# State space stage of a two-block network: the recurrence of two groups at once in complex pairs

## The chip, the cores and the metric

The kernel runs on one core of one Trainium2 chip. The metric is the device time of the program in microseconds, and the kernel before is given as the median of 3 runs. The program has one core, so the slowest core is that core.

## The reference

The network has an attention block and a state space block, each with a normalization behind it, and further parts in the same program. The change lies in the state space block (S5). Its reference, cut to what is computed there:

```python
E_BRANCH, S5_GROUP, S5_GROUPS, S5_STATE, S5_CHUNK = 2048, 16, 128, 64, 128

def _s5_direction(u_ctx, u_lat, lam, dt, bmat, cmat):
    lam_dt = lam * dt[:, None]
    lam_bar = jnp.exp(lam_dt)
    b_bar = ((lam_bar - 1.0) / lam)[..., None] * bmat
    ...
    def step(h, u_chunk):
        bu = jnp.einsum('btgs,gps->btgp', u_chunk.astype(jnp.complex64), b_bar)
        a = jnp.broadcast_to(lam_bar, bu.shape)
        _, xs = lax.associative_scan(_ssm_combine, (a, bu), axis=1)
        xs = xs + powers[None] * h[:, None]
        y = jnp.einsum('btgp,gsp->btgs', xs, cmat).real
        return xs[:, -1], y
    ...
    h_ctx, y_ctx = run(u_ctx, h0)
    _, y_lat = run(u_lat, h_ctx)

def _s5_mixer(h_lat, h_ctx, w_in, ...):
    u_l, g_l = jnp.split(h_lat @ w_in, 2, axis=-1)
    u_c, g_c = jnp.split(h_ctx @ w_in, 2, axis=-1)
    ...
    y = jax.nn.gelu(y)
    ya, yb = jnp.split(y @ w_glu + b_glu, 2, axis=-1)
    return ((ya * jax.nn.sigmoid(yb)) * jax.nn.silu(g)) @ w_out
```

For two directions a linear recurrence x(t) = lam x(t-1) + B u(t) with complex lam runs over 256 context tokens and goes on over 256 latent tokens (backwards for the second direction), and only the latents' output is wanted.

## The kernel before

The kernel does the recurrence in steps of 8 tokens, so a direction has 32 columns of context and 32 of latents. The 2048 channels lie in four rounds or groups b = 0 to 3 of 16 blocks of operators, worked in four parts a = 0 to 3 of 1 MB each. For a round:

- **Linears.** `u` computes 128 columns of the input branch for context and latents (48 matmuls; a weight part is split into a high and a low half, `weight`: a load on SyncE, a cast on ScalarE at L97, a difference on VectorE at L98). `s5_store_u` copies the result with ScalarE (`s_ut`, L438), turned so that 8 tokens lie in a column, and stores it to DRAM (`d_u`); `s5_load_u` reads it back as U (L446) with another partition order. The first round's U is read on SyncE, the others' on GpSimd's queue.
- **Blocks.** `s5_blocks` multiplies U by the operators `d_rt` (matmuls `vps`, L472, 256 a round), and ScalarE copies each of 8 results to V (L475), which holds [real/imaginary][direction][16 rows][64 columns] on 128 partitions.
- **Scan.** `s5_scan` is VectorE's part: a tree of five levels over the context's columns (the first in two halves), then 7 steps of 4 columns and 3 steps of 8 over the latents, with a table of powers of lam (`s5_steps`, L332 to L337). A step is two products (L493), one sum (L495), one difference (L496), one sum (L497). At the end the second direction's columns are turned (L517).
- **Out.** `s5_out` multiplies U ("within", L536, operators `d_t`) and the states V ("across", L549, operators `d_o`), transposes (`ytps`, L560), and ScalarE does the gelu (L1096). The gates (`lin`, 24 matmuls each) are linears whose silu is stored for later.

TensorE and VectorE run in the order in which the code is written. `s5_layer` writes it: round b's scan is handed out in pieces (`run(scan, us)`) beside the linears of later rounds, the gates, and the within and across products of round b-1; then the blocks of round b+1 come, and the next scan. Operators lie in a ring of five 1 MB tiles, loaded on GpSimd's queue; weight parts in a ring of two (high and low). Behind the stage, `ya` in two halves feeds the GLU's linears.

## Time and profile before

| | us |
|---|---|
| median of 3 runs | 1450.82 |
| lowest and highest | 1448.18, 1453.40 |
| profiled execution, its own time | 1449.68 |
| span of the trace | 1447.9 |
| TensorE busy, whole span | 1328.2 (92%) |
| VectorE busy, whole span | 1150.6 (79%) |
| ScalarE busy, whole span | 712.2 (49%) |

The profile is of one execution. The span is what the trace covers of that execution's own time. Busy shares are means over stages that differ: in the state space stage, some 240 of the 1448 us, VectorE and TensorE both have a large share, and which of them sets the end is read from that stage alone.

### The profile page before, as it was taken

To read this page: it belongs to the slowest core of one execution; us is meant where nothing else is said; L and a number is where in the kernel's file an instruction comes from. 1 tells how busy PE (TensorE), PEld (TensorE's weight loads), DVE (VectorE), ACT (ScalarE), POOL (GpSimd) and SP (SyncE) were. 2 spreads that over 40 slices of the span, in tenths; PEclk is the share of its full clock that TensorE was granted. 3 is DMA by queue.
4 is the path that set the end of the run, shared out by engine and by line. 5 is a ranking of instruction groups with operands and counts; after the bars stand their busy time and mean duration, and the time that the engine had idled before them with its cause. 6 is when DMAs were issued, how large, how long until landed. Compare 5 with 4: busy or idle time off the path is not lost.

```text
span 1447.9 us, 31095 instructions
## 1 busy us (share of the span) xinstructions
PE 1328.2 (92%) x12512; PEld 1196.9 (83%) x12512; DVE 1150.6 (79%) x2123; ACT 712.2 (49%) x1308; POOL 102.9 (7%) x225
## 2 busy tenths in 40 slices
PE   5879979999999988988768699999999999999997
PEld 4656657888888887888757599999998999999996
DVE  7999888998888899389898766555578876888887
ACT  4424436765656536322333264444347556655554
POOL 0012221111001100111111000000000000000000
PEclk9989988999999998999898899999999999999999
DMA  9469996665455544797778665655555453555552
GB/s 347 165 197 282 294 280 168 183 178 157 156 159 158 163 124 154 236 315 256 256 269 298 252 228 181 209 196 193 189 166 180 154 182 103 179 188 188 189 183 96
DMA packets 140625, 291.40 MB, mean 201 GB/s; under 512 B 30480, under 2 KB 70080, under 8 KB 135104
## 3 DMA queue, kind: packets, MB, share of 16 engines
q1 hardware_dynamic: 108592, 232.01, 48.2%
q0 software_dynamic: 11360, 49.34, 10.9%
q10 hardware_dynamic: 20528, 8.06, 2.1%
q8 instruction: 98, 1.61, 0.4%
q14 instruction: 47, 0.39, 0.1%
HBM read 234.83 MB, written 54.53 MB: 200 GB/s over the span
## 4 chain that ended last, share of the span: by engine, by line
PE 67%; DVE 20%; DMA 7%; issue 3%; ACT 3%; SPq 0%; DVEq 0%; ACTq 0%
PE lin L120 14%; PE lin L121 14%; PE lin L119 14%; DVE s_t L493 4%; DVE wl L98 3%; PE vps L472 2%; DVE s_V L495 2%; DMA sp_x<-in_s_bcw_dram 2%; DVE sp_t L37 2%; DMA mraw<-in_w_mod_dram 1%; PE dn L121 1%; PE dn L119 1%; PE dn L120 1%; DMA d_o<-sp_o 1%; DVE s_V L497 1%
## 5 line engine op out<-in xcount | busy, mean ns | idle before, releaser
L97 ACT CAST wh<-wr 128x1024 fp32r<-128x1024 f32 x268 | 280.7, 1049 | 405.4 <-PE lin L120 258.0
L98 DVE TENSOR_TENSOR wl<-wr,wh 128x1024 fp32r<-128x1024 f32 x268 | 327.6, 1223 | 146.3 <-ACT wh L97 145.6
L119 PE MATMUL lin<-prH,wh 128*128 128x256 f32 x512 | 145.3, 284 | 0.0
L119 PE MATMUL lin<-yaH,wh 128*128 128x256 f32 x512 | 144.9, 283 | 0.0
L120 PE MATMUL lin<-yaL,wh 128*128 128x256 f32 x512 | 144.7, 283 | 0.0
L121 PE MATMUL lin<-prH,wl 128*128 128x256 f32 x512 | 143.7, 281 | 1.0 <-DVE wl L98 1.0
L120 PE MATMUL lin<-prL,wh 128*128 128x256 f32 x512 | 144.1, 281 | 0.4 <-DVE prL L109 0.2
L121 PE MATMUL lin<-yaH,wl 128*128 128x256 f32 x512 | 144.2, 282 | 0.0
L120 PEld LDWEIGHTS lin<-prL,wh 128*128 128x128 f32 x512 | 96.6, 189 | 2.1 <-DVE prL L109 1.0
L119 PEld LDWEIGHTS lin<-yaH,wh 128*128 128x128 f32 x512 | 97.6, 191 | 0.0
L121 PEld LDWEIGHTS lin<-yaH,wl 128*128 128x128 f32 x512 | 97.5, 190 | 0.0
L119 PEld LDWEIGHTS lin<-prH,wh 128*128 128x128 f32 x512 | 96.7, 189 | 1.0
L120 PEld LDWEIGHTS lin<-yaL,wh 128*128 128x128 f32 x512 | 97.4, 190 | 0.0
L121 PEld LDWEIGHTS lin<-prH,wl 128*128 128x128 f32 x512 | 96.2, 188 | 1.2 <-DVE wl L98 1.2
L493 DVE TENSOR_TENSOR s_t<-s_V,s_tab 128x256 f32<-128x256 f32 (+2 forms) x120 | 73.1, 652 | 16.0 <-ACT s_V L475 14.7
L121 PE MATMUL u<-h,wl 128*128 128x256 f32 x224 | 64.1, 286 | 9.7 <-DVE wl L98 9.6
L121 PE MATMUL lin<-h,wl 128*128 128x256 f32 x128 | 43.2, 338 | 32.2 <-DVE wl L98 32.2
L427 POOL DMA_DIRECT2D d_t<-sp_g x128 | 67.0, 531 | 59.6 <-DVE sp_g L37 55.4
L119 PE MATMUL u<-h,wh 128*128 128x256 f32 x224 | 64.0, 286 | 0.0
L120 PE MATMUL u<-h,wh 128*128 128x256 f32 x224 | 63.3, 283 | 0.0
L119 PE MATMUL lin<-hH,wh 128*128 128x512 f32 x144 | 60.9, 423 | 0.7 <-ACT hH L103 0.7
L37 DVE TENSOR_TENSOR sp_t<-s_pb,sp_x 128x1024 f32<-128x1024 f32 x64 | 59.9, 953 | 0.6
(505 smaller groups left out, 3837.2 us busy)
## 6 DMA issues: line engine op xcount, KB each, us to landing
wr<-in_glu_dram SPq DMA_DIRECT2D x64, 512.0 KB, 3.3
wr<-in_w_up_dram SPq DMA_DIRECT2D x44, 512.0 KB, 3.3
wr<-in_w_in_dram SPq DMA_DIRECT2D x32, 512.0 KB, 4.8
mraw<-in_w_mod_dram SPq DMA_DIRECT2D x64, 256.0 KB, 3.3
d_rt<-sp_rt SPq DMA_DIRECT2D x64, 256.0 KB, 4.1
d_o<-sp_o SPq DMA_DIRECT2D x32, 512.0 KB, 4.7
wr<-in_s_in_dram SPq DMA_DIRECT2D x32, 512.0 KB, 4.4
s_op<-d_o POOLq DMA_DIRECT2D x16, 1024.0 KB, 7.3
```

Of the source, the lines that this page charges most:

```text
L37: return lambda *a, **k: self.net.in_order(f(*a, **k))
L97: self.in_order(nc.scalar.copy(hi, raw))
L98: self.in_order(nc.vector.tensor_tensor(lo, raw, hi.bitcast(F32), SUB))
L119: self.in_order(t.matmul(out, a[0], b[0], start=start, stop=False))
L120: self.in_order(t.matmul(out, a[0], b[1], start=False, stop=False))
L121: self.in_order(t.matmul(out, a[1], b[0], start=False, stop=stop))
L427: nc.gpsimd.dma_start(self.d_t[k].rearrange("s i j e c -> i s j e c")[:, :, j, e], a)
L472: self.in_order(nc.tensor.matmul(p[64 * e:64 * e + 64, c:c + 64], rt[:, d, j, r, 64 * e:64 * e + 64], u, start=True, stop=True, skip_group ...
L493: go(v.tensor_tensor(t[:, x], src.to_broadcast([128, 2, 32, n]), a[x].unsqueeze(1).to_broadcast([128, 2, 32, n]), MUL))
L495: go(v.tensor_tensor(dst, dst, t[:, 0], ADD))
L497: go(v.tensor_tensor(dst[:, 1], dst[:, 1], t[:, 1, 0], ADD))
```

## The change

- V holds pairs: real and imaginary part of a state lie side by side. The context's columns go to a tile C of the group, the latents' 31 columns and a start column to V of a pair of groups; ScalarE copies each block's result in two pieces (L476, L477), and turns the second direction in doing so.
- The context tree is one per group (`s5_context`): four levels, then one step for the last column only. The latents (`s5_latents`) go column by column, 31 steps, for two groups at once. A step (`s5_step`) is four operations, each on the result of the one before: product with the real part (L483), sum (L484), product of the swapped pair with the signed imaginary part (L483), sum (L484). The table of powers shrinks to doublings.
- The linears of rounds 1 to 3 and the gates come from one list (`linear`); weight parts are fetched two ahead while inputs are computed, every second one into a spare tile (`wx`). U is loaded on SyncE for all rounds, between the weight parts; the turned copy `s_ut` has one buffer instead of two; the operators' ring has four tiles instead of five.
- The order is made by two clocks, one of TensorE (`clock[0]`) and one of VectorE (`clock[1]`), that a table of costs moves on. What it makes on TensorE: one linear, then blocks(0,0) and so on, a linear and a block in turn to blocks(0,3); a linear; within(0) with a linear in it; blocks(1,0), a linear, blocks(1,1) to (1,3); then a linear and a part of blocks(2) in turn; three linears (the last input one and two gates), blocks(3) with a gate; across(0), across(1) and within(1) to (3) with gates between; behind the scan's end across(2) and across(3). Before, two linears came ahead of the four blocks of round 0, and across(3) alone stood behind the scan's end.

On VectorE, at the start of the scan. Before (`s_V` are the states, `wl` the low half of a weight part):

```order
L493 TENSOR_TENSOR s_t<-s_V,s_tab 128x512 x2
L495 TENSOR_TENSOR s_V<-s_V,s_t 128x64x8
L496 TENSOR_TENSOR s_V<-s_V,s_t 128x32x8
L497 TENSOR_TENSOR s_V<-s_V,s_t 128x32x8
L493 TENSOR_TENSOR s_t<-s_V,s_tab 128x512 x2
L495 TENSOR_TENSOR s_V<-s_V,s_t 128x64x8
L496 TENSOR_TENSOR s_V<-s_V,s_t 128x32x8
L497 TENSOR_TENSOR s_V<-s_V,s_t 128x32x8
L98 TENSOR_TENSOR wl<-wr,wh 128x1024
L493 TENSOR_TENSOR s_t<-s_V,s_tab 128x512 x2
L495 TENSOR_TENSOR s_V<-s_V,s_t 128x64x8
L496 TENSOR_TENSOR s_V<-s_V,s_t 128x32x8
```

and now, where group 1's context ends and the latents of groups 0 and 1 begin (`s_lam` and `s_li` are lam's parts):

```order
L483 TENSOR_TENSOR s_t<-s_C,s_tr 128x64
L484 TENSOR_TENSOR s_V<-s_C,s_t 128x2x16x2
L483 TENSOR_TENSOR s_t<-s_C,s_ti 128x64
L484 TENSOR_TENSOR s_V<-s_V,s_t 128x2x16x2
L483 TENSOR_TENSOR s_t<-s_V,s_lam_579 128x128
L484 TENSOR_TENSOR s_V<-s_V,s_t 128x2x32x2
L483 TENSOR_TENSOR s_t<-s_V,s_li 128x128
L484 TENSOR_TENSOR s_V<-s_V,s_t 128x2x32x2
L100 TENSOR_TENSOR wx<-wr,wx 128x1024
L483 TENSOR_TENSOR s_t<-s_V,s_lam_579 128x128
L484 TENSOR_TENSOR s_V<-s_V,s_t 128x2x32x2
L483 TENSOR_TENSOR s_t<-s_V,s_li 128x128
```

The steps of the latents have one column instead of four or eight, and weight parts (now L100) stand between them at other places.

On SyncE, behind the first operators. Before (`in_s_in` is the input weight, all of round 1 to 3's U loads stood on GpSimd's queue):

```order
L96 DMA wr<-in_s_in_dram 128x1024
L451 DMA s_op<-d_rt 128x2048 x2
L446 DMA s_U<-d_u 128x512 x4
L451 DMA s_op<-d_rt 128x2048 x2
L96 DMA wr<-in_s_in_dram 128x1024 x19
L96 DMA wr<-in_glu_dram 128x1024 x5
```

and now:

```order
L456 DMA s_op<-d_rt 128x2048 x2
L451 DMA s_U<-d_u 128x512
L98 DMA wr<-in_s_in_dram 128x1024 x3
L451 DMA s_U<-d_u 128x512
L98 DMA wr<-in_s_in_dram 128x1024 x2
L451 DMA s_U<-d_u 128x512 x2
L98 DMA wr<-in_s_in_dram 128x1024
L451 DMA s_U<-d_u 128x512
L98 DMA wr<-in_s_in_dram 128x1024
L451 DMA s_U<-d_u 128x512
L98 DMA wr<-in_s_in_dram 128x1024
L451 DMA s_U<-d_u 128x512
```

The U loads of rounds 1 to 3 stand between the weight parts.

On ScalarE at the end of the stage (`s_ysb` are a group's products, `y` the gelus, `yaH` their high half, `wh` the high half of a weight part). Before:

```order
L1096 ACTIVATE y<-ytps 128x128 x8
L1128 CAST yaH<-y 128x512 x2
L556 COPY s_ysb<-yps 128x32x16 x2
L97 CAST wh<-wr 128x1024
L1096 ACTIVATE y<-ytps 128x128 x8
L97 CAST wh<-wr 128x1024
L1128 CAST yaH<-y 128x512 x2
```

and now:

```order
L1158 ACTIVATE y<-ytps 128x128 x8
L1163 CAST yaH<-y 128x512 x2
L558 COPY s_ysb<-yps 128x32x16 x2
L1158 ACTIVATE y<-ytps 128x128 x8
L99 CAST wh<-wr 128x1024
L1163 CAST yaH<-y 128x512 x2
L99 CAST wh<-wr 128x1024 x2
```

The first GLU weight's cast stood ahead of the last eight gelus and stands behind them. And where linear (2,3) is turned and stored, ScalarE has the cast of the next weight part ahead of the turned copy.

The diff, cut to its core:

```diff
+    def s5_turn_u(self, ps, tp, bufs=2):
+        ut = tp.tile([128, 8, 2, 32], F32, name="s5_ut", bufs=bufs)
         for seg in range(2):
-            nc.scalar.copy(ut[:, :, 1 - seg, :], ps[:, seg * 256:seg * 256 + 256].rearrange("p (k s) -> p s k", s=8))
-        nc.scalar.dma_start(self.d_u[b, j].rearrange("s p k -> p s k")[:, ::-1], ut.rearrange("p s g k -> p s (g k)"))
-
-    def s5_load_u(self, b, j, tp, queue=None):
-
-        nc = self.nc
-        if j == 0:
-            self.U[b] = tp.tile([128, 4, 8, 64], F32, name="s5_U", bufs=3)
-        (queue or nc.gpsimd).dma_start(self.U[b][:, j].rearrange("p q k -> p (q k)"),
-                                       self.d_u[b, j].rearrange("s (i q) k -> (s i) (q k)", q=8))
+            self.nc.scalar.copy(ut[:, ::-1, 1 - seg, :],
+                                ps[:, seg * 256:seg * 256 + 256].rearrange("p (k s) -> p s k", s=8))
+        return ut
+    def s5_store_u(self, b, j, ps, tp, bufs=2):
+        self.nc.scalar.dma_start(self.d_u[b, j].rearrange("s p g k -> p s (g k)"),
+                                 self.s5_turn_u(ps, tp, bufs).rearrange("p s g k -> p s (g k)"))
+    def s5_load_u(self, b, j, U):
+        self.nc.sync.dma_start(U[:, j].rearrange("p q g k -> p (q g k)"),
+                               self.d_u[b, j].rearrange("s (i q) g k -> (s i) (q g k)", q=8))
...
-        t = self.ops.tile([128, 2048], F32, name="s5_op", bufs=5)
+        t = self.ops.tile([128, 2048], F32, name="s5_op", bufs=4)
...
-                nc.scalar.copy(V[:, :, d, 4 * a:4 * a + 4, :].rearrange("p r q k -> p r (q k)"),
-                               p.rearrange("p (r c) -> p r c", r=2))
...
-        def step(a, src, dst):
-
-            n = dst.shape[-1]
-            t = T[:, :, :, :, 0:n]
-            for x in range(2):
-                go(v.tensor_tensor(t[:, x], src.to_broadcast([128, 2, 32, n]),
-                                   a[x].unsqueeze(1).to_broadcast([128, 2, 32, n]), MUL))
-            go(v.tensor_tensor(dst, dst, t[:, 0], ADD))
-            go(v.tensor_tensor(dst[:, 0], dst[:, 0], t[:, 1, 1], SUB))
-            go(v.tensor_tensor(dst[:, 1], dst[:, 1], t[:, 1, 0], ADD))
...
+            pv = p.rearrange("p (r q k) -> p r q k", r=2, q=4)
+            c, x = (t[:, 4 * a:4 * a + 4].rearrange("p q k r -> p r q k") for t in (C[:, d], V[:, d, b % 2]))
+            nc.scalar.copy(c[:, :, :, ::-1] if d else c, pv[:, :, :, 0:32])
+            nc.scalar.copy(x[:, :, :, 1 - d:32 - d], pv[:, :, :, 32 + d:63 + d])
+    def s5_step(self, a, src, swapped, t, base, dst):
+        v = self.nc.vector
+        for x, y, z in ((src, a[0], base), (swapped, a[1], dst)):
+            self.in_order(v.tensor_tensor(t, x, y.to_broadcast(t.shape), MUL))
+            self.in_order(v.tensor_tensor(dst, z, t, ADD))
+    def s5_column(self, V, c, b=None, swap=False):
+        return bass.AP(tensor=V.tensor, offset=V.offset + 2 * c[0] + 1024 * (b or 0) + swap,
+                       ap=[V.ap[0], [2048 + 2 * (c[1] - c[0]), 2], [64, 32 if b is None else 16], [1 - 2 * swap, 2]])
+    def s5_context(self, b, C, V, tp):
+        Cf = C.rearrange("p d q k r -> p (d q) k r")
+        t = tp.tile([128, 1024], F32, name="s5_t")
+        for l in range(4):
             h, m = 1 << l, 2 << l
-            for c in (range(0, 32, 16) if l == 0 else (0,)):
-                e = c + 16 if l == 0 else 32
-                step(power(h), Vf[:, :, :, c + h - 1:e:m], Vf[:, :, :, c + m - 1:e:m])
-                yield 0.6 + 0.27 * ((e - c) // m)
-
-        for k in range(7):
-            step(power(1), Vf[:, :, :, 31 + k:63:8], Vf[:, :, :, 32 + k:63:8])
-            yield 1.5
-        for k in range(39, 63, 8):
-            step([self.tab[:, x, b] for x in range(2)], Vf[:, :, :, k - 1:k], Vf[:, :, :, k:k + 8])
-            yield 2.5
-
-        for r in range(2):
-            go(v.tensor_copy(V[:, r, 1, :, 0:31], V[:, r, 1, :, 62:31:-1]))
-        yield True
-
-    def s5_out(self, b, UVS, tp, emit):
+            a = self.tr[:, b, l].unsqueeze(2).unsqueeze(3), self.ti[:, b, l].unsqueeze(2)
+            i, o = slice(h - 1, 32, m), slice(m - 1, 32, m)
+            x, n = Cf[:, :, o], 32 // m
+            self.s5_step(a, Cf[:, :, i], Cf[:, :, i, ::-1],
+                         t[:, 0:64 * n].rearrange("p (c k r) -> p c k r", c=32, r=2), x, x)
+            yield 0.7 + 0.27 * n
+        x, base = (C[:, :, :, k] for k in (15, 31))
+        a = (self.tr[:, b, 4].rearrange("p (d c) -> p d c", d=2).unsqueeze(3),
+             self.ti[:, b, 4].rearrange("p (d c) r -> p d c r", d=2))
+        self.s5_step(a, x, x[:, :, :, ::-1], t[:, 0:64].rearrange("p (d c r) -> p d c r", d=2, r=2), base,
+                     self.s5_column(V, (0, 31), b % 2))
+        yield 0.9
+    def s5_latents(self, g, V, tp):
+        t = tp.tile([128, 1024], F32, name="s5_t")[:, 0:128].rearrange("p (d c r) -> p d c r", d=2, r=2)
+        a = (self.lam8[:, 0].rearrange("p (d c q) -> p d c q", d=2, c=2)[:, :, g].unsqueeze(3),
+             self.li[:, g].rearrange("p (d c) r -> p d c r", d=2))
+        for k in range(31):
+            c, o = (k, 31 - k), self.s5_column(V, (k + 1, 30 - k))
+            self.s5_step(a, self.s5_column(V, c), self.s5_column(V, c, swap=True), t, o, o)
+            yield 1.18
...
+                while len(parts) < n and asked[0] < len(linears):
+                    k, x = asked[0], linears[asked[0]]
+                    place = None
+                    if k < 12 and k % 2 == 1:
+                        place = [spare[:, k // 2 % 2, i] for i in range(2)]
+                    parts.append(self.weight(I["s5_in"][16 + x if isinstance(x, int) else 4 * x[0] + x[1]],
+                                             place=place))
+                    asked[0] += 1
+                    clock[1] += 1.3
...
+            def linear():
+                n = asked[0] - len(parts)
+                fetch(1)
+                w, x = parts.pop(0), linears[n]
+                fetch(2 if n < 10 else 1)
+                if isinstance(x, int):
+                    p = self.ps("lin")
+                    self.products(p[:, 0:256], w, (h1[0][:, 0], h1[0][:, 1]))
+                    sg = tp.tile([128, 256], F32, name="s5_sg", bufs=2)
+                    nc.scalar.activation(sg, p[:, 0:256], AF.Silu)
+                    nc.scalar.dma_start(self.d_sg[x][:, 0:256], sg)
+                    beside(2.9)
+                else:
+                    b, j = x
+                    if j == 0:
+                        U[b] = tp.tile([128, 4, 8, 2, 32], F32, name="s5_U", bufs=3)
+                    self.s5_store_u(b, j, self.u(w, h1), tp, 1)
+                    self.s5_load_u(b, j, U[b])
+                    beside(5.8)
...
+                if a == 3:
+                    clock[1] = max(clock[1], clock[0] + 1.0) if not jobs else clock[1]
+                    jobs.append(self.s5_context(b, C[b], V[b // 2], tp))
+                    if b % 2 == 1:
+                        jobs.append(self.s5_latents(b // 2, V[b // 2], tp))
...
+            U[0] = tp.tile([128, 4, 8, 2, 32], F32, name="s5_U", bufs=3)
+            for j in range(4):
+                self.s5_load_u(0, j, U[0])
+            ahead = [self.operator(self.d_rt[a], nc.sync) for a in range(4)]
+            self.ordered = (mybir.EngineType.PE, mybir.EngineType.DVE)
+            for a in range(4):
+                linear()
+                if a == 1:
+                    self.s5_steps(tp)
+                    clock[1] += 4.5
+                blocks(0, a)
+            linear()
+            within, across, close = out(0)
+            for a in range(4):
+                within(a)
+                if a == 1:
+                    linear()
+            blocks(1, 0)
+            linear()
+            for a in range(1, 4):
+                blocks(1, a)
+            first = jobs[-1]
+            for a in range(4):
+                linear()
+                blocks(2, a)
+            for _ in range(3):
+                linear()
+            for a in range(4):
+                blocks(3, a)
+                if a == 2:
+                    linear()
+            last = jobs[-1]
+            scanned(first)
...
+            scanned(last)
             ya.append(self.big.tile([128, 16, 256], F32R, tag="s16", name="yaL", bufs=3))
             for a in range(4):
                 across(a)
-                if a < 3:
+                if a < 2:
                     low(a)
             close()
+            high(2)
+            for a in range(4):
+                final[1](a)
+            low(2)
+            final[2]()
```

## Rows read from the trace of the kernel before

**Rows 1.** The table of stretches of the stage: start and end, length, then for each engine the busy time and the number of its instructions, then the granted TensorE clock as a share of full speed (1.00 is 2.4 GHz, 0.50 is 1.2 GHz), the busy share of the DMA engines, and GB/s.
```profile
599.80:611.40 11.60, 11.60 (x98) 11.48 (x96) 3.70 (x8) 3.68 (x8) 0.00 (x0) 1.00 0.74 259
...
625.70:660.00 34.30, 29.29 (x239) 28.54 (x237) 33.67 (x65) 7.97 (x15) 3.12 (x6) 1.00 0.82 285
...
711.00:716.00 5.00, 5.00 (x27) 4.78 (x28) 4.90 (x11) 0.38 (x1) 0.00 (x0) 0.50 0.42 152
```

**Rows 2.** The chain of waits of 600 to 850 us, followed back from the last instruction and printed in order of time: start, length, what.
```profile
601.51 6.41 DMA d_u<-s_ut
609.36 5.06 DMA s_U<-d_u
614.46 7.03 PE vps L472 x186
...
625.71 1.29 DVE s_t L493 x2
...
664.53 7.97 PE vps L472 x256
...
825.42 2.71 issue
```

**Rows 3.** VectorE's instructions of 600 to 845 us by line and shape: count, busy time in us and mean ns of one, then the idle time ahead of them and what ended it.
```profile
L493 DVE TENSOR_TENSOR s_t<-s_V,s_tab 128x256 f32<-128x256 f32 x64 | 36.3, 610 | 0.8
L493 DVE TENSOR_TENSOR s_t<-s_V,s_tab 128x512 f32<-128x512 f32 x48 | 34.2, 754 | 15.1 <-ACT s_V L475 14.7
L98 DVE TENSOR_TENSOR wl<-wr,wh 128x1024 fp32r<-128x1024 f32 x27 | 32.9, 1219 | 18.1 <-ACT wh L97 18.1
...
L517 DVE COPY s_V<-s_V 128x496 f32<-128x496 f32 x8 | 3.2, 438 | 0.0
```

**Rows 4.** The timeline of VectorE at the start of the stage: start, length, line, operation, out<-in, shape, count (a row of x2 gives the length of both together).
```profile
611.26 0.43 DVE L332 TENSOR_TENSOR s_t<-s_tab 128x256 f32<-128x256 f32 x1
...
619.06 0.40 DVE L335 TENSOR_TENSOR s_t<-s_tab 128x128 f32<-128x128 f32 x1
...
628.32 1.28 DVE L493 TENSOR_TENSOR s_t<-s_V,s_tab 128x512 f32<-128x512 f32 x2
...
632.06 2.05 DVE L493 TENSOR_TENSOR s_t<-s_V,s_tab 128x512 f32<-128x512 f32 x2
```

**Rows 5.** The timeline of VectorE early in the program: small contiguous operations, the second row six in a row of which each reads what the one before wrote.
```profile
20.82 0.28 DVE L37 TENSOR_TENSOR lm_sz<-lm_em 128x128 f32<-128x128 f32 x1
...
28.04 1.92 DVE L37 SCALAR_TENSOR_TENSOR lm_er<-lm_er,lm_sz 128x128 f32<-128x128 f32 x6
```

**Rows 6.** A group of line 37, in the operators' preparation: count, duration in ns min/median/max, first and last start; contiguous tiles.
```profile
L37 DVE TENSOR_TENSOR sp_x<-sp_x x16: 416/425/427, 49.4 to 541.6; 128x256 f32<-128x256 f32 x16
```

**Rows 7.** The timeline of ScalarE at the start of the stage (a row with ACTq is a DMA that ScalarE issues).
```profile
599.88 1.05 ACT L97 CAST wh<-wr 128x1024 fp32r<-128x1024 f32 x1 [4.17 <-PE u L120]
600.84 0.64 ACT L438 COPY s_ut<-u 128x256 f32<-128x256 f32 x2
601.51 0.37 ACTq L439 DMA_DIRECT2D d_u<-s_ut  x1
...
625.09 0.59 ACT L475 COPY s_V<-vps 128x512 f32<-128x512 f32 x1 [0.35 <-PE vps L472]
```

**Rows 8.** The timeline of SyncE's issues at the start of the stage.
```profile
608.04 1.75 SPq L446 DMA_DIRECT2D s_U<-d_u  x4
```

**Rows 9.** DMA issues of 640 to 800 us: count, KB of each, median us from issue to landing.
```profile
s_op<-d_o POOLq DMA_DIRECT2D x12, 1024.0 KB, 7.2
...
wr<-in_s_in_dram SPq DMA_DIRECT2D x15, 512.0 KB, 5.6
...
s_U<-d_u POOLq DMA_DIRECT2D x10, 256.0 KB, 4.5
d_u<-s_ut ACTq DMA_DIRECT2D x8, 256.0 KB, 3.3
```

**Rows 10.** All issues on the branch's DRAM tile from 595 to 845 us, stores and loads together: the spread from issue to landing.
```profile
DMA to landing us min/median/max: 2.3/4.6/11.7
```

**Rows 11.** Waits of 595 to 845 us: who waited, for whom, us in total, times, longest.
```profile
PE lin L121 <- DVE wl L98: 29.2, 10, 6.4
DVE wl L98 <- ACT wh L97: 26.9, 5, 10.0
...
DVE s_t L493 <- ACT s_V L475: 14.7, 4, 6.6
```

**Rows 12.** The timeline of all engines at the end of the stage (POOL L451 issues an operator's load).
```profile
822.05 0.74 DVE L517 COPY s_V<-s_V 128x496 f32<-128x496 f32 x2
...
822.40 1.96 PE L536 MATMUL yps<-s_op,s_U 128*32 128x128 f32 x64
...
823.81 0.53 POOL L451 DMA_DIRECT2D s_op<-d_o  x1 [2.72 <-PE yps L536]
...
824.28 1.14 PE L549 MATMUL yps<-s_op,s_V 64*32 64x128 f32 x62
...
834.75 1.07 ACT L556 COPY s_ysb<-yps 128x512 f32<-128x512 f32 x2 [8.80 <-PE yps L549]
...
837.03 2.07 ACT L1096 ACTIVATE y<-ytps 128x128 f32<-128x128 f32 x8 [0.26 <-PE ytps L560]
...
837.50 0.56 PE L119 MATMUL lin<-yaH,wh 128*128 128x256 f32 x1
```

234 lines of the change are left out of this document (99 added, 135 removed).

## The prediction

> **What bounds the kernel now.** I read the table of stretches first, since the change lies in one stage: 599.8 us (last input linear of the stage before) to 837.5 us (first matmul of the GLU) [rows 1, 12]. While the scan runs VectorE is full (33.67 of 34.30 us) and TensorE is not (29.29) [rows 1]. The chain of waits agrees: it runs over VectorE's scan from 625.71 us, leaves it only for a round's four blocks of 8 us, when the scan waits for ScalarE's copies of them, and ends in TensorE's last products [rows 2]. VectorE's idle time has two large parts: 26.9 us for the casts of weights and 14.7 us for those copies [rows 11]. So the stage is a start of 25.9 us (599.8 to 625.7), a VectorE chain of 197.1 us (to 822.79, the end of the last L517), and a tail of 14.7 us [rows 12]. I price each of the three in the new order.
>
> **VectorE's scan.** Three kinds of rows set the price of one operation. Contiguous: 128 elements take 0.28 us, six dependent ones 1.92, so 0.32 each from start to start [rows 5]; 256 take 0.425 [rows 6]; 1024 take 1.22 [rows 3]. On a line through these an operation is about 0.155 us and 1.04 ns an element, and 0.03 us more if it waits for the one before: 0.25, 0.32, 0.455, 0.72 and 1.25 us for 64, 128, 256, 512 and 1024. Single elements 16 or 32 bytes apart are dearer: L493 on 256 has a mean of 0.610 [rows 3], on 512 at the second level 1.02 each, against 0.64 at the first, where the elements are 8 bytes apart [rows 4]. Runs of two at 32 bytes cost what contiguous ones do: the second doubling of the powers' table, 256 elements, 0.43 [rows 4]. The new code reads complex pairs, so nearly all of its operations are of the last kind; that, not their number (328 before and after), is what it gains.
> A group's context is now four levels and a last step of four operations each: 4 x (1.25 + 0.72 + 0.455 + 0.32 + 0.25) = 12.0 us, for four groups 47.9. The latents are 31 steps of 4 x 0.32 = 1.28 us for two groups at once: 39.7, for both pairs 79.4. Together 127.3 us. The powers' table gets cheaper too (some 11 to 5 us), at nothing: it lies in time in which VectorE has no other work.
>
> **The start.** Before, two linears (11.6 us) run while the first inputs U go through DRAM, then four blocks without a gap. Now one linear is ahead (5.8 us), and the other three stand between the blocks. The inputs land at 614.4 us as before, because their last store (601.51 + 6.41) and load (609.36 + 5.06) [rows 2] are not touched. From there four blocks of 2.0 (664.53, 7.97 for four) and three linears of 5.8 [rows 1] make 25.4 us, to 639.8. TensorE idles 8.8 us ahead of that, from 605.6; after such a gap rows show half the clock for a while (0.50 from 711 to 716 [rows 1], after a wait for blocks), and 5 us at half clock lose 2.5: 642.3. With the copies of the last block (0.59 and the issue between, [rows 7]) the first context scan starts at 643.5, against 625.7: **+17.8 us**. It is not lost work, since these linears are wanted later; but VectorE has nothing to do meanwhile.
>
> **The chain after it.** VectorE's order is written out, so I follow it against TensorE's. Context 0 with two weight parts, and a third part (1.22 each), ends at 659.3. Context 1 needs blocks(1,3); TensorE has until then three linears, the four "within" products (1.9, [rows 12]) and four blocks: 27.3 us from 642.3, to 669.6. **10.6 us idle.** Context 1 with its part ends at 683.2, and the 31 steps of pair 0 begin, with weight parts between them.
> TensorE meanwhile ends linear (2,3) at 675.4 and stands before blocks(2,0), which need it back from DRAM. ScalarE now casts a weight part first (1.05), then turns (0.65) and stores (0.37 to issue) [rows 7]; the store lands after 3.3 to 6.4 us, SyncE issues the load (0.44, [rows 8]), which lands after 4.5 to 5.1 [rows 2, 9]. That is 10.3 to 14.0 us; the middle puts blocks(2,0) at 687.5. Before, two or more linears stood between such a pair. Blocks and linears (2.0 and 5.8) follow in turn, with half the clock at first: linear (3,2) ends near 711, blocks(2,3), linear (3,3) and the first gate (2.9) near 723. Each of these two frees the buffer of a weight part whose cast VectorE's order puts between steps of the latents. VectorE gets there at about 708 and 715 and waits 4.5 and 9.9 us: **14.4 us**. Then nothing is late: the rest of pair 0 ends at 742, contexts 2 and 3 with three parts at 769.5, pair 1 with four parts at 814.
> As a sum: 643.5 + 127.3 + 16 parts x 1.2 + 10.6 + 14.4 less about 1 of overlap = **814**, against 822.8. The chain shrinks by 26.6 us, and 17.8 of these are taken by the start.
> ScalarE copies a block in two pieces for one of 0.59; at 0.37 a piece (its copies of 256 take 0.32 each, [rows 7]) it stays under a block's 1.0 us of TensorE, so this is hidden. Should it not be, 32 x 0.15 us would come in part to the wait for blocks: 2 us at most. The interleaved write and the step of 8 bytes with which TensorE now reads the states have no row; from 0 to 2 us, I take 0.
>
> **The tail.** The scan of groups 2 and 3 now ends together, so two groups' "across" products stand behind it instead of one. The ring of 1 MB operators has four slots instead of five, all with group 2's; group 3's are issued only as across(2) frees slots, 1.14 us each [rows 12]. If each lands as fast as one alone (7.2 us [rows 9]), the last is there 11.8 us after the scan's end; at the 285 GB/s of the full queues [rows 1] 4 MB take 14.7, and it is there after 15.8. I take 14.5, since four stand at once. Then 1.14 of products, 2.28 of copies and transposes (834.75 to 837.03) less some 0.4 beside the last products, 2.07 of gelus [rows 12], and the first GLU weight's cast (1.05), which ScalarE's order now has behind the gelus: **20.6 us** (19 to 22.5) instead of 14.7, **+5.9**. Group 2's gelus fall under the loads.
>
> **Sum.** +17.8 - 26.6 + 5.9 = -2.9 us. The profiled execution took 1449.68 us, 1.14 below the median of the three runs, and -2.9 makes 1446.8 of it and 1447.9 of the median: **1447**. Outside the stage nothing changes but the tile shape of the branch's stores.
>
> **A rule that says otherwise.** The rows show 10 us and more from a linear's end to its inputs' return, 3.3 to 6.4 and 4.5 to 5.1 of it landings. The Trainium skill ("DMA: Bandwidth & Descriptors", Anatomy of one DMA) gives a transfer a fixed 2.0 us and its bytes at 436 GB/s, which makes an estimate of 2.6 us for these 256 KB; by it the sum would be some 4 us lower, and the trace, with its queues busy, does not agree. The rows decide the sum.
>
> **Rivals.**
> (A) *Faster: the way through DRAM is short and steps are cheap.* The new stores and loads have runs of 256 bytes or longer in both directions as before, but the loads move from GpSimd's queue to SyncE's, and the smallest landing of either is 2.3 us [rows 10]. With a landing of 3.3 and one of 2.3 blocks(2,0) start at 683.5, and what VectorE waits in pair 0 shrinks as much: -4.0. If a dependent step is 0.30 an operation instead of 0.32 (0.28 is the duration), the 31 steps of pair 1, which nothing covers, give -2.5, and the tail at its lower end -1.6. With all three 1438.7, with the first alone 1442.8. Against it: in this stage landings this short are the exception.
> (B) *Slower: SyncE's queue holds the weights back.* SyncE now issues each U load in line with the weight parts, and a load waits for its store; the parts behind it wait too, and VectorE waits in order for them, in the midst of the scan. From a linear's end it is 1.05 + 0.65 + 0.37 and the store's landing until SyncE is free, then 5.6 to land a part [rows 9], 1.05 to cast and 1.22. Two parts ahead cover two linears and two blocks, 15.6 us. So the store's landing decides: from 5.6 us on each part is late. The median is 3.3 [rows 9], the first one 6.4, the longest of the tile 11.7 [rows 10]. At 6.4 it is 0.8 a linear, at 11.7 it is 6 us; with a few long ones among eight linears, +6 to +12: 1453 to 1459. For it: VectorE and TensorE wait for parts before too (26.9 and 29.2 us [rows 11]).
> (C) *Much slower: the pairs do not run at the full rate.* The swapped operand is read backwards in twos, 256 bytes apart. At the rate of singles a step is 4 x 0.42 (128 elements, 0.40 and 0.03 [rows 4]) = 1.68 us, 62 steps cost 25 us more: 1471. Against it: the pairs of rows 4, and L517, which reads 496 elements backwards in 0.438 us [rows 3].
> The Trainium skill ("SBUF — State Buffer", Door 1: The DMA port swizzle, its note on cachelines) has 16-byte lines that want two accesses each; that agrees with the pairs at 0.43 and the singles at 0.61, and by it (C) falls away. No row here shows pairs read backwards.
>
> **How the numbers follow.** The measurement tells about 0.3% (4.35 us) from no change, so faster means below 1446.5 and slower above 1455.2. The sum's case (1442 to 1452, its stalls good to some 5 us): 0.45, nearly half of it below 1446.5. (A) 0.26, all faster. (B) 0.20, most of it slower. (C) 0.05. The rest, 0.04, on the slow side. Faster 0.46, same 0.31, slower 0.23. The range is from below (A)'s lower end, where the stall of 14.4 would also shrink by a few us, to (B)'s upper end: 1435 to 1460.
>
> **What would show it.** In the profile after: the first context operation at 643 (not 626); an operation on 128 pairs' elements in 0.28 to 0.30, a step in 1.2 to 1.3; VectorE idle about 10 us ahead of context 1 and at two weight parts in the latents of pair 0, for casts; TensorE idle 10 us ahead of blocks(2,0); the scan's end near 814, and some 20 us from there to the GLU, with group 3's operators landing last. Wrong would be steps of 1.6 us (C), weight parts that wait for loads behind SyncE's U loads (B), or blocks(2,0) within 8 us of linear (2,3) (A).

## The result, and the profile after

The changed kernel takes 1464.81 us (median of 6 runs, 1459.38 to 1465.95) against 1449.50 of the kernel before: ratio 1.0093, 95% interval 1.0069 to 1.0117. It is slower by some 13 us by the ratio; 1447, about no change, was forecast, and 1464.81 lies above the range's end of 1460. A second set of the same kernel (e9 below) gave 1.0080 (1.0053 to 1.0107). One experiment's profiled execution (e1's) had a mean granted clock of 0.829, where the others had 0.950 to 0.968, and no points are read from it.

The profiled execution took 1464.20 us, its span is 1462.4 us. The table of stretches of the stage, cut at 611.4 us as in [rows 1], the first context, context 1, 730 us, TensorE's last gate, the scan's end and the first GLU matmul (columns as in [rows 1]; a row is left out):

```profile
599.80:611.40 11.60, 5.68 (x48) 5.48 (x46) 2.36 (x2) 3.85 (x12) 0.00 (x0) 0.96 0.74 254
611.40:646.50 35.10, 31.07 (x420) 29.82 (x421) 8.17 (x23) 12.22 (x38) 2.53 (x4) 0.87 0.83 292
646.50:676.00 29.50, 27.88 (x465) 26.68 (x464) 14.68 (x23) 9.78 (x26) 3.17 (x6) 1.00 0.86 274
676.00:730.00 54.00, 41.88 (x518) 40.70 (x517) 38.47 (x101) 13.05 (x32) 2.12 (x4) 0.87 0.68 220
...
798.70:826.30 27.60, 0.24 (x3) 0.03 (x1) 20.79 (x69) 1.43 (x2) 0.00 (x0) 0.55 0.31 122
826.30:848.60 22.30, 14.66 (x528) 12.08 (x529) 3.67 (x6) 7.03 (x18) 2.11 (x4) 0.73 0.58 211
```

The start is longer: VectorE is busy for 8.17 us of the 35.1 to 646.5, and for 14.68 of the next 29.5. The same columns for 625.7 to 676 us alone, where VectorE's first scan ran before; of the kernel before:

```profile
625.70:676.00 50.30, 44.67 (x543) 43.42 (x542) 49.22 (x94) 13.98 (x25) 6.00 (x11) 0.97 0.79 271
```

and of the changed kernel, VectorE at work for 17.14 us of 50.3 instead of 49.22:

```profile
625.70:676.00 50.30, 48.68 (x775) 46.88 (x774) 17.14 (x25) 18.26 (x46) 4.98 (x9) 1.00 0.84 275
```

The last stretches of the first table show the other side: TensorE has ended everything that it may do at 798.7 and stands idle for 27.6 us until the scan is over.

VectorE's operations by line and shape, 640 to 830 us (columns as in [rows 3]), answer to those rows:

```profile
L484 DVE TENSOR_TENSOR s_V<-s_V,s_t 128x128 f32<-128x128 f32 x124 | 36.4, 293 | 4.2
L100 DVE TENSOR_TENSOR wl<-wr,wh 128x1024 fp32r<-128x1024 f32 x15 | 18.3, 1221 | 17.0 <-ACT wh L99 16.9
L483 DVE TENSOR_TENSOR s_t<-s_V,s_li 128x128 f32<-128x128 f32 x62 | 18.2, 293 | 2.1
...
L484 DVE TENSOR_TENSOR s_C<-s_C,s_t 128x1024 f32<-128x1024 f32 x8 | 9.8, 1228 | 0.3
L484 DVE TENSOR_TENSOR s_C<-s_C,s_t 128x512 f32<-128x512 f32 x8 | 5.6, 695 | 0.3
```

An operation on 128 elements takes 0.293 us, on 512 0.695, on 1024 1.228: close to what the contiguous rows gave for 128 and 1024 (0.28 in [rows 5], 1.22 in [rows 3]) and to the 0.69 that their line gives for 512. The swapped pairs (`s_li`) take no longer than the others. The scan is as cheap as forecast. What it waits for stands in VectorE's timeline (the bracket is the idle time ahead and what ended it). First the start of context 0, its last step, and the start of context 1:

```profile
646.51 1.23 DVE L483 TENSOR_TENSOR s_t<-s_C,s_tr 128x1024 f32<-128x1024 f32 x1 [10.09 <-ACT s_C L476]
...
663.87 0.23 DVE L484 TENSOR_TENSOR s_V<-s_C,s_t 128x64 f32<-128x64 f32 x1 [4.02 <-ACT s_V L477]
...
676.03 1.23 DVE L483 TENSOR_TENSOR s_t<-s_C,s_tr 128x1024 f32<-128x1024 f32 x1 [10.27 <-ACT s_C L476]
```

Then, in the same view, two weight parts in the latents of the first pair:

```profile
718.68 1.23 DVE L100 TENSOR_TENSOR wl<-wr,wh 128x1024 fp32r<-128x1024 f32 x1 [3.90 <-ACT wh L99]
...
729.52 1.23 DVE L100 TENSOR_TENSOR wl<-wr,wh 128x1024 fp32r<-128x1024 f32 x1 [8.43 <-ACT wh L99]
```

And a weight part in the latents of the second pair, and the scan's last operation. The first line is ScalarE's: the cast of that part, which waits for a weight of the GLU to land:

```profile
804.47 1.04 ACT L99 CAST wh<-wr 128x1024 fp32r<-128x1024 f32 x1 [4.85 <-DMA wr<-in_glu_dram]
...
805.55 1.23 DVE L100 TENSOR_TENSOR wl<-wr,wh 128x1024 fp32r<-128x1024 f32 x1 [4.60 <-ACT wh L99]
...
825.98 0.29 DVE L484 TENSOR_TENSOR s_V<-s_V,s_t 128x128 f32<-128x128 f32 x1
```

The scan ends at 825.98 + 0.29 = 826.27 us. Behind it, GpSimd's timeline has the loads of group 3's four operators, here the first and the last:

```profile
828.65 0.53 POOL L456 DMA_DIRECT2D s_op<-d_o  x1 [32.25 <-PE yps L551]
...
832.38 0.53 POOL L456 DMA_DIRECT2D s_op<-d_o  x1 [0.37 <-PE yps L551]
```

and TensorE's timeline the products that wait for them, up to the first GLU matmul:

```profile
840.72 1.53 PE L551 MATMUL yps<-s_op,s_V 64*32 64x128 f32 x48 [1.10 <-DMA s_op<-d_o]
843.41 2.39 PE L551 MATMUL yps<-s_op,s_V 64*32 64x128 f32 x80 [1.15 <-issue]
847.01 1.97 PE L562 MATMUL ytps<-ident,s_ysb 128*128 128x128 f32 x8 [1.21 <-ACT s_ysb L558]
848.63 0.56 PE L121 MATMUL lin<-yaH,wh 128*128 128x256 f32 x1
```

A piece of group 3 is 64 products. The third piece starts at 840.72, when its load lands (issued at 831.49, 9.2 us); the fourth's load, issued at 832.38, lands after 10.7 us, and the last 80 products start at 843.41. So the stage ends at 848.63, 22.4 us behind the scan. That first GLU matmul doesn't wait for group 3's gelus, nor for the cast that stands behind them (ScalarE's timeline):

```profile
848.16 2.05 ACT L1158 ACTIVATE y<-ytps 128x128 f32<-128x128 f32 x8 [1.20 <-PE ytps L562]
849.99 1.07 ACT L99 CAST wh<-wr 128x1024 fp32r<-128x1024 f32 x1
```

So the stage is 46.7 us to the first context, a chain of 179.8 and a tail of 22.4, where it was 25.9, 197.1 and 14.7: +20.8, -17.3 and +7.7 make +11.1 us (848.63 - 837.50 = 11.13). The span differs by 14.5. The other 3.4 lie behind the stage: 1.1 in the GLU's first stretch, which begins after TensorE's idle time at a lower clock (0.83 over its first 12 us; 0.93 before), and some 2.3 in later stages, in which the clock fell where it didn't before (0.94 from 1108.6 to 1168.6 us, 1.00 in the same stretch before). The stage's order does not reach those, and no run here isolates them.

### The profile page after: what moved, and what is told of

The parts are those of the page before. It is cut to its first block, busy times and chain, and to the rows that moved or that the text cites. A ratio compares the mean times of both kernels' runs of the same rounds, so it can differ in the third digit from the quotient of the medians.

```text
span 1462.4 us, 31168 instructions
## 1 busy us (share of the span) xinstructions
PE 1322.6 (90%) x12512; PEld 1193.8 (82%) x12512; DVE 1104.9 (76%) x2119; ACT 715.7 (49%) x1354; POOL 95.9 (7%) x213
## 4 chain that ended last, share of the span: by engine, by line
PE 65%; DMA 13%; DVE 12%; issue 6%; ACT 3%; SPq 0%; POOL 0%; DVEq 0%; ACTq 0%; POOLq 0%
PE lin L122 14%; PE lin L121 14%; PE lin L123 14%; DMA d_u<-s_ut 4%; DMA sp_x<-in_s_bcw_dram 3%; DVE sp_t L37 2%; DMA d_o<-sp_o 2%; DVE wl L100 2%; DMA mraw<-in_w_mod_dram 1%; PE dn L123 1%; PE dn L121 1%; PE dn L122 1%; DVE sp_r L37 1%; PE u L121 1%; PE u L122 1%
## 5 line engine op out<-in xcount | busy, mean ns | idle before, releaser
L99 ACT CAST wh<-wr 128x1024 fp32r<-128x1024 f32 x262 | 274.4, 1048 | 358.9 <-PE lin L122 242.1
L100 DVE TENSOR_TENSOR wl<-wr,wh 128x1024 fp32r<-128x1024 f32 x262 | 320.4, 1224 | 168.6 <-ACT wh L99 167.8
L122 PE MATMUL lin<-yaL,wh 128*128 128x256 f32 x512 | 145.4, 284 | 0.0
L429 POOL DMA_DIRECT2D d_t<-sp_g x128 | 66.8, 529 | 60.0 <-DVE sp_g L37 55.7
L37 DVE TENSOR_TENSOR sp_t<-s_pw,sp_x 128x1024 f32<-128x1024 f32 x64 | 59.8, 954 | 0.8
L551 PE MATMUL yps<-s_op,s_V 64*32 64x128 f32 x1024 | 22.4, 321 | 41.8 <-DVE s_V L484 32.5
L470 PE MATMUL vps<-s_U,s_op 128*64 128x64 f32 x1024 | 37.2, 235 | 23.7 <-DMA s_U<-d_u 16.5
L122 PE MATMUL lin<-hL,wh 128*128 128x512 f32 x144 | 57.6, 400 | 0.5 <-DVE hL L106 0.5
L123 PE MATMUL lin<-hH,wl 128*128 128x512 f32 x144 | 57.4, 399 | 0.0
```

Source lines behind the costliest of these rows:

```text
L37: return lambda *a, **k: self.net.in_order(f(*a, **k))
L99: self.in_order(nc.scalar.copy(hi, raw))
L100: self.in_order(nc.vector.tensor_tensor(lo, raw, hi.bitcast(F32), SUB))
L122: self.in_order(t.matmul(out, a[0], b[1], start=False, stop=False))
L123: self.in_order(t.matmul(out, a[1], b[0], start=False, stop=stop))
L429: nc.gpsimd.dma_start(self.d_t[k].rearrange("s i j e c -> i s j e c")[:, :, j, e], a)
```

## The experiments

Every time is a ratio to the kernel before on the same chip, with its 95% interval; the points of the stage are read from each run's profiled execution.

| run | ratio | first context | context 1 | scan's end | first GLU matmul | tail |
|---|---|---|---|---|---|---|
| before | 1 | 625.7 (first scan) | - | 822.8 | 837.5 | 14.7 |
| changed | 1.0093 (1.0069 to 1.0117) | 646.5 | 676.0 | 826.3 | 848.6 | 22.4 |
| e9, changed again | 1.0080 (1.0053 to 1.0107) | 647.3 | 677.1 | 826.3 | 846.0 | 19.6 |
| e1, two places to turn | 1.0042 (1.0021 to 1.0062) | | | | | |
| e10, the same again | 1.0043 (1.0029 to 1.0058) | 648.5 | 675.9 | 825.5 | 845.3 | 19.8 |
| e2, a linear ahead of blocks(2) | 1.0033 (1.0010 to 1.0057) | 647.1 | 676.9 | 822.4 | 843.4 | 21.1 |
| e3, GLU parts behind the scan | 1.0040 (1.0015 to 1.0065) | 645.2 | 675.3 | 819.3 | 842.7 | 23.4 |
| e4, last operators held | 1.0044 (1.0025 to 1.0062) | 646.1 | 674.7 | 825.5 | 841.9 | 16.5 |
| e11, U loads on GpSimd | 1.0087 (1.0059 to 1.0115) | 651.6 | 682.2 | 831.6 | 852.6 | 20.9 |
| e5, two places, start as before | 1.0034 (1.0012 to 1.0056) | 629.0 | 670.2 | 818.1 | 837.8 | 19.7 |
| e6, e1 to e4 together | 0.9945 (0.9926 to 0.9963) | 645.6 | 673.0 | 808.2 | 824.5 | 16.3 |
| e7, e6 with the start as before | 0.9912 (0.9882 to 0.9941) | 629.5 | 670.1 | 807.0 | 823.0 | 16.1 |
| e8, e7 with blocks(1) early | 0.9928 (0.9895 to 0.9961) | 630.4 | 668.0 | 810.1 | 827.6 | 17.5 |

In the traces that start as the changed kernel does, the first inputs land between 616.6 and 620.2 us (616.8 in the changed kernel's, 619.5 in e9's, 620.2 in e10's), so a point can move by some 3 us without an edit. Distances within a row are firmer.

The theory: the scan's own work is as cheap as forecast, and its gain is spent in three places, each of which can be taken away alone: TensorE's waits for inputs on their way through DRAM, GLU weight parts in the last latents, and group 3's operators behind a full ring; the later first scan costs only as much as TensorE's work comes later. The rivals: the U loads in SyncE's queue hold the weights back, or the later start is itself the loss.

**e9.** No edit.

> The changed kernel itself, beside the two runs that follow. Theory and rival alike: ratio 1.007 to 1.012 to the kernel before.

It was met.

**e1 and e10, two places for the turned copy.**

```diff
+        if bufs == 1:
+            self.turn = 1 - self.turn
+            ut = self.both[:, 512 * self.turn:512 * self.turn + 512].rearrange("p (s g k) -> p s g k", s=8, g=2)
...
-            ysb = tp.tile([128, 8, 4, 2, 16], F32, name="s5_ysb", bufs=1)
+            ysb = self.both.rearrange("p (t a e s) -> p t a e s", t=8, a=4, e=2)
```

> The turned copy of a linear gets two places instead of one (in the tile that the products' copy uses later); nothing else is changed. In the changed kernel ScalarE waits 13.5 us in all for a store to land before it may turn the next linear, and the store of linear (2,2) takes 11.9 us. Theory (the way through DRAM paces TensorE, and so the two late weight parts in the latents of the first pair): blocks(2,0) start some 6 to 8 us earlier, the waits of 3.9 and 8.4 us shrink by as much, and the time falls by 5 to 8 us, to about 1457 to 1460. Rival (the landing itself, not the single place, holds the inputs back): the turn goes earlier, but the store lands as late as before behind the one ahead, and the time changes by less than 2 us.

> Two places for the turned copy, a second time, for a trace at the usual clock. Theory: blocks(2,0) start 4 to 8 us earlier than in the changed kernel (692.8), the weight parts in the latents of pair 0 come as much earlier, and the scan ends 4 to 7 us earlier; ratio 1.002 to 1.006. Rival (the landing itself holds the inputs back): blocks(2,0) start less than 2 us earlier, and the time is that of the changed kernel.

Both sets are 5 to 7 us below the changed kernel (1.0042 and 1.0043 against 1.0080 and 1.0093). In the changed kernel the chain of waits runs from store to store here, and linear (2,3)'s turn waits for the store of linear (2,2) (start, length, what):

```profile
652.37 9.64 DMA d_u<-s_ut
...
662.77 9.16 DMA d_u<-s_ut
672.68 11.85 DMA d_u<-s_ut
...
685.29 4.75 DMA d_u<-s_ut
690.06 2.67 DMA s_U<-d_u
692.77 3.04 PE vps L470 x52
```

ScalarE's timeline has the turn:

```profile
684.61 0.65 ACT L440 COPY s_ut<-u 128x256 f32<-128x256 f32 x2 [3.85 <-DMA d_u<-s_ut]
```

The store issued at 672.68 lands at 684.53, and the turn starts at 684.61. With two places no turn waits for a store in e10's trace, but it shows less than the theory's 4 to 8 us: blocks(2,0) wait until 691.0 instead of 693.3 in e9, and from the first context to the scan's end it is 177.0 us instead of 179.0. The two late weight parts stay, against the theory (VectorE's timeline of e10):

```profile
717.95 1.22 DVE L100 TENSOR_TENSOR wl<-wr,wh 128x1024 fp32r<-128x1024 f32 x1 [3.29 <-ACT wh L99]
...
728.80 1.23 DVE L100 TENSOR_TENSOR wl<-wr,wh 128x1024 fp32r<-128x1024 f32 x1 [8.44 <-ACT wh L99]
```

What the second place gives lies ahead of context 1: from the first inputs' landing to context 1 it is 55.7 us instead of 59.2 (57.6 in e9), and from there to the scan's end 149.5 instead of 150.2 (149.2). The times fell by more than the 2 to 4 us that these executions show; how the rest divides is open.

**e2, one more linear ahead of blocks(2).**

```diff
+            linear()
             for a in range(4):
                 linear()
                 blocks(2, a)
-            for _ in range(3):
+            for _ in range(2):
```

> One more linear stands ahead of blocks(2,0), so two linears are under way while linear (2,3)'s inputs go through DRAM; the turned copy has one place as in the changed kernel. Theory (TensorE's idle time ahead of blocks(2), 15 us in the changed kernel, is what makes the two weight parts late): 5.8 us of it are filled, the part's wait of 8.4 us falls below 3, and the time falls by 5 to 8 us. Rival (VectorE's own work sets the end, and what TensorE gains is only waited for elsewhere): the scan's end moves by less than 2 us and so does the time.

The time fell by 7 to 9 us and the scan's end by 3.9. One of the two waits in the first latents is gone, the other stays at 7.73 us (VectorE's timeline):

```profile
725.68 1.23 DVE L100 TENSOR_TENSOR wl<-wr,wh 128x1024 fp32r<-128x1024 f32 x1 [7.73 <-ACT wh L99]
```

From context 1 to the scan's end it is 145.4 us instead of 150.2 (149.2 in e9). The rival is out by the time; the theory had the wait of 8.4 fall below 3, and the size in the trace is that of one wait, not of both.

**e3, the GLU's parts behind the scan.**

```diff
             scanned(last)
+            self.early = [self.weight(x) for x in list(I["glu"][16])]
...
-            self.products(p[:, :n], self.weight(s), tuple(a[:, 8 * i:8 * i + 8] for a in act),
+            self.products(p[:, :n], self.early.pop(0) if self.early else self.weight(s), tuple(a[:, 8 * i:8 * i + 8] for a in act),
```

> The two differences of the first GLU weight, which VectorE's order has among the last latents, stand behind the scan's end; nothing else is changed. Theory (they are part of the chain that sets the end: a wait of 4.6 us for the weight to land and two operations of 1.2): the scan ends 6 to 7 us earlier and the time falls by 6 to 7 us. Rival (the tail waits for the GLU's weight instead): the scan's end moves, but the first GLU matmul doesn't, and the time changes by less than 2 us.

The scan's end moved from 826.27 to 819.30, 7.0 us, and the two differences stand behind the last step and wait for nothing (VectorE's timeline):

```profile
819.01 0.29 DVE L484 TENSOR_TENSOR s_V<-s_V,s_t 128x128 f32<-128x128 f32 x1
819.22 2.35 DVE L100 TENSOR_TENSOR wl<-wr,wh 128x1024 fp32r<-128x1024 f32 x2
```

This trace's first context is 1.4 us early, so the distance from context 2's start (747.28 us) to the scan's end is the better measure: 72.0 us, where it is 78.9 in the changed kernel and 77.7 in e9, 6 to 7 us less. The first GLU matmul moved by 6.0 (3.3 against e9), and the time fell by 6 to 8 us. The rival is out.

**e4, the last operators held.**

```diff
+        def held(a):
+            t = tp.tile([128, 2048], F32, tag="s5_C" if a < 2 else "s5_U", name="s5_oph", bufs=2 if a < 2 else 3)
+            nc.gpsimd.dma_start(t, self.d_o[b * 4 + a])
+            return t
...
+            two = [self.operator(self.d_o[8 + a]) for a in range(4)]
+            three = [final[3](a) for a in range(4)]
             scanned(last)
...
-                across(a)
+                across(a, two[a])
...
-                final[1](a)
+                final[1](a, three[a])
```

> The last group's four operators are loaded ahead of the scan's end into tiles that are dead by then (two context tiles, two input tiles) instead of into the ring behind group 2's products. Theory (the tail of 22.5 us from the scan's end to the first GLU matmul is the load of 4 MB through a full ring): the tail falls to some 12 us (two groups' products 8 to 10, copies, transposes and gelus 4, less what overlaps), and the time falls by 8 to 11 us. Rival (products at half clock, gelus and the weight's cast make up the tail): less than 4 us.

The tail is 16.5 us: less than the changed kernel's 22.4 and 19.6, more than the 12 expected. TensorE's timeline behind the scan has no wait for a load left; 256 products take 5.60 us:

```profile
825.53 5.60 PE L556 MATMUL yps<-s_op,s_V 64*32 64x128 f32 x256 [26.44 <-DVE s_V L484]
832.29 1.09 PE L567 MATMUL ytps<-ident,s_ysb 128*128 128x128 f32 x8 [1.16 <-ACT s_ysb L563]
833.31 2.69 PE L556 MATMUL yps<-s_oph,s_V 64*32 64x128 f32 x176
837.76 1.38 PE L556 MATMUL yps<-s_oph,s_V 64*32 64x128 f32 x80 [1.75 <-issue]
840.30 1.97 PE L567 MATMUL ytps<-ident,s_ysb 128*128 128x128 f32 x8 [1.16 <-ACT s_ysb L563]
841.92 0.56 PE L121 MATMUL lin<-yaH,wh 128*128 128x256 f32 x1
```

So the load of 4 MB through the full ring is some 3 to 6 us of the tail, not 8 to 11, and the two groups' products with their copies and transposes are the rest, as the rival had it in part. The time is 5 to 7 us below the changed kernel, between the theory's 8 to 11 and the rival's 4.

**e11, U loads on GpSimd's queue.**

```diff
-                    self.s5_load_u(b, j, U[b])
+                    self.s5_load_u(b, j, U[b], nc.gpsimd)
```

> The inputs of rounds 1 to 3 are loaded on GpSimd's queue again, between the operators, as in the kernel before; one place for the turned copy. Rival (B) of the prediction (U loads on SyncE hold the weight parts back): the waits for weights of 3.9, 8.4 and 4.6 us fall by half or more and the time falls by 6 us or more. Theory (the weight parts wait for their buffer, that is for TensorE, and not for SyncE): the waits stay, and the time changes by less than 3 us, or rises, where an operator's load now stands behind a store.

The waits for weight parts are 4.14, 8.44 and 3.69 us, as in e9 (4.07, 8.43, 3.50), and the time is that of the changed kernel. The rival (B) of the prediction falls. The first context of this trace starts 4 to 5 us later, and the time doesn't show it.

**e5, the start as before, with two places.**

```diff
-            for a in range(4):
-                linear()
-                if a == 1:
-                    self.s5_steps(tp)
-                    clock[1] += 4.5
-                blocks(0, a)
-            linear()
+            linear()
+            linear()
+            self.s5_steps(tp)
+            clock[1] += 4.5
+            for a in range(4):
+                blocks(0, a)
+            for a in range(3):
+                linear()
```

> Two places for the turned copy, and at the stage's start the order of the kernel before: two linears, then blocks(0,0) to (0,3) without a linear between, then the linears. The first context scan starts where it started before. Theory (VectorE's 20.8 us later start are lost only as far as TensorE's work comes later too; between the first scan and the second group's blocks VectorE waits for TensorE anyway): the first scan starts near 627, some 19 us earlier, but the wait ahead of context 1 grows from 10 to about 20 us, context 1 starts 6 to 9 us earlier than in the run with two places alone, because 5.8 us of TensorE's idle time and its half clock are filled, and the time is 5 to 9 us below that run (ratio about 0.998 to 1.001 to the kernel before). Rival (the later start is the loss itself): the whole chain moves by 15 us or more and the time comes out below 0.995 of the kernel before.

The first context starts 19.5 us earlier than in e10, and the wait ahead of context 1 grows from 10.5 to 15.1 us (VectorE's timeline):

```profile
628.98 1.22 DVE L487 TENSOR_TENSOR s_t<-s_C,s_tr 128x1024 f32<-128x1024 f32 x1 [8.06 <-ACT s_C L480]
...
637.14 1.23 DVE L100 TENSOR_TENSOR wx<-wr,wx 128x1024 fp32r<-128x1024 f32 x1 [3.16 <-ACT wx L99]
...
653.92 1.22 DVE L100 TENSOR_TENSOR wx<-wr,wx 128x1024 fp32r<-128x1024 f32 x1 [5.28 <-ACT wx L99]
670.22 1.22 DVE L487 TENSOR_TENSOR s_t<-s_C,s_tr 128x1024 f32<-128x1024 f32 x1 [15.08 <-ACT s_C L480]
```

Context 1 starts 5.7 us earlier, just under the theory's 6 to 9, and the wait is short of its 20. The ratio, 1.0034 against 1.0043, shows no gain that can be told from none, where 5 to 9 us were expected. The runs spread over 12 us, and the profiled one (1449.98 us) is among the shortest, so the 7.4 us at the scan's end in its trace are more than the typical run gains. The rival, 15 us and more, is out.

**e6 and e7, together.** The diffs are those above.

> The four edits together: two places for the turned copy, one more linear ahead of blocks(2), the GLU's two differences behind the scan, the last group's operators held in dead tiles; the start is that of the changed kernel. Theory (each removes another piece of the chain): the chain after the start loses 4 to 8 us by the first two together, which act on the same idle time, 7 us by the third, the tail 6 us by the fourth: 17 to 21 us below the changed kernel, ratio 0.994 to 0.998 to the kernel before. Rival (they remove the same time, since each gave some 7 us alone): 8 to 10 us, ratio 1.002 or more.

> The four edits and the start of the kernel before (two linears, then four blocks). Theory: as the run with the four edits, and 5 to 9 us below it; ratio 0.989 to 0.994 to the kernel before. Rival (with the four edits VectorE is the bound from the first scan on): 15 us below it.

e6 is 20 us below the changed kernel (0.9945 against 1.0080 to 1.0093): the pieces that gave 23 to 31 us one by one give 20 to 21 together, so most of each is its own, and the rival's 8 to 10 are out. e7 has the lowest ratio, 0.9912, some 13 us below the kernel before. It is 5 us below e6, at the low end of the theory, and the two intervals overlap. Its first context starts 16.1 us ahead of e6's, its scan ends 1.2 us ahead.

**e8, blocks(1) early.**

```diff
             for a in range(4):
                 within(a)
-                if a == 1:
-                    linear()
-            blocks(1, 0)
-            linear()
-            for a in range(1, 4):
+            for a in range(4):
                 blocks(1, a)
             first = jobs[-1]
-            linear()
+            for a in range(3):
+                linear()
```

> As the run before this one, but the blocks of group 1 stand ahead of the linears of round 2 (two linears, blocks(0), three linears, within(0), blocks(1), four linears, then blocks(2) and linears in turn). Theory (VectorE's wait ahead of context 1 is TensorE's work that need not stand there): context 1 starts near 651 instead of 663 to 668, the latents of pair 0 end earlier, and unless blocks(2) and (3) are then late the scan ends 8 to 12 us earlier: ratio 0.981 to 0.988 to the kernel before. Rival (TensorE and the way through DRAM pace the stage from there on, so blocks(3) end no earlier): the wait moves to contexts 2 and 3, and the time changes by less than 3 us.

Context 1 starts at 668.0, not at 651: with fewer linears between, blocks(1) wait for their own way through DRAM (TensorE's timeline), and later parts come late too.

```profile
657.23 9.13 PE L474 MATMUL vps<-s_U,s_op 128*64 128x64 f32 x228 [7.47 <-DMA s_U<-d_u]
```

The time is that of e7 within the intervals, as the rival had it. Its reason is not quite the one seen: the waits move to the latents of the second pair (1.40, 3.68 and 2.54 us at weight parts from 768 to 785 us), not to contexts 2 and 3.

## Why the prediction was wrong

**The scan's price was right.** 0.293 us an operation and 0.33 from start to start against 0.32; 1.228 and 0.695 for the contexts. Rival (C) did not occur: a pair read backwards takes 0.293 us on 128 elements, a pair read forwards 0.292. The Trainium skill ("SBUF — State Buffer", Door 1: The DMA port swizzle) wants two accesses to each 16-byte line for the full rate; the runs agree.

**The start was right in kind:** 646.5 instead of 643.5. The first inputs landed 2.4 us later than in the execution before (616.83: 610.85 and 5.98), and TensorE ended the four blocks 1.9 us later (644.2 instead of 642.3). The other 1.1 are the copies of the last block, which stand behind a turn that waits 1.60 us for a store.

**The chain failed**, at the sentence "Then nothing is late", and at a wait for which the sum has no term. It was summed from 643.5 as 170.5 us and took 179.8, 9.3 more. Up to context 1 it was 3.1 us more (29.5 instead of 26.4, 643.5 to 669.9), from there on 6.1 (150.2 instead of 144.1).

The 3.1 us belong to the turned copy's single place, in large part. ScalarE may turn a linear only when the store of the one before has landed, and it waits 13.5 us in all for that; the copies of the blocks stand behind it (ScalarE's timeline):

```profile
644.72 0.65 ACT L440 COPY s_ut<-u 128x256 f32<-128x256 f32 x2 [1.60 <-DMA d_u<-s_ut]
...
662.09 0.65 ACT L440 COPY s_ut<-u 128x256 f32<-128x256 f32 x2 [4.04 <-DMA d_u<-s_ut]
...
672.00 0.65 ACT L440 COPY s_ut<-u 128x256 f32<-128x256 f32 x2 [3.45 <-DMA d_u<-s_ut]
```

The second of these holds up context 0's last step (its 4.02), the third the copies for context 1: TensorE has ended blocks(1,3) at 673.85, and the context starts at 676.03. TensorE also waits 1.32 us for inputs ahead of these blocks. With two places (e10) the turns don't wait, and the way from the first inputs to context 1 is 2 to 4 us shorter. The change names the one place, and the sum gives its wait no price.

Of the 6.1 us, 6 to 7 are the GLU's first weight parts: the sum counted 16 parts of 1.2 us, VectorE's order has 18 behind the first context, and the last waits 4.6 us for a weight to land. e3, which moves just these two, gives 6 to 7 us back. The code keeps VectorE's order for the stage alone, so these rows of the next stage's code may stand among the stage's; following the stage's list misses them. Another 1.7 us are steps at 0.33. On the other side the waits of 3.9 and 8.4 us were forecast as 4.5 and 9.9, 2.1 more than measured.

**The tail came out near in part by luck:** 20.6 forecast, 22.4 (19.6 in e9) measured, with errors that offset each other. The loads are as described but later: they went out 2.4 to 6.1 us behind the scan's end, and the last was there after 16.8 us, not 14.5. The last products, copies and transposes took 5.5 us, at a granted clock of 0.50, where 3.0 were summed. On the other side the sum had 2.07 us of gelus and 1.05 of a cast ahead of the first GLU matmul, which waits for neither: it starts 0.5 us into the gelus, as it did before (gelus from 837.03, matmul at 837.50 in [rows 12]). e4 shows that the load behind the full ring is only 3 to 6 us of the tail.

From 834.6, the stage's end as summed, to 848.6 it is 14.0 us: 3.0 the start, 9.3 the chain, 1.8 the tail. Another 3.4 lie behind the stage, where no term stood at all.

**Where the expected gain went.** The scan's operations were busy for 170.6 us (all groups of lines 493 to 517, the largest in [rows 3]) and are now for 118.6 (all of lines 483 and 484): 52 us less, and e7, in which most of the losses are taken away, is 13 us below the kernel before; that its gain comes from these 52 is argued, since no run has the old scan in e7's order. But the new scan starts the latents only when two groups' blocks are there, and puts linears between the blocks. By 676 us VectorE had done 17 us of work in 50 (from 625.7) where it did 49. That loss isn't the late first scan: e5 and e7 start it 16 to 20 us earlier, and gain 3 to 6 us at context 1 and 1 us (e7 against e6) to 7 us (e5 against e10) at the scan's end. It is the wait for the second group, which is TensorE's own work (27.88 of 29.5 us busy) and the way through DRAM; e8 brought context 1 only 2 us forward. Rival (A) did not occur: the stores issued from 601 to 686 us landed after 4.8 to 11.9 us. The Trainium skill ("DMA: Bandwidth & Descriptors", Anatomy of one DMA) has a fixed 2.0 us and the bytes at 436 GB/s for a DMA that GpSimd issues; taken over to these stores, which ScalarE issues, that is the estimate of 2.6 us, and only those from 703 us on come near it, with 2.4 to 4.0.

What stays open: why e1's and e10's times fell by 5 to 7 us when the traces show 2 to 4, and the 2.3 us in later stages.
